# One decoder block on one core: a row normalization taken off GpSimd, row stores moved to GpSimd's queue, one gather ahead of a conditional part, and extra products without readers

## The chip, the cores and the metric

The kernel runs on one core of a Trainium2 chip. The metric is the device time in microseconds of one execution. Times inside an execution are counted from the start of its span. TensorE does matrix products and transposes, VectorE (DVE), ScalarE (ACT) and GpSimd (POOL) work on rows, SyncE (SP) issues most transfers; GpSimd issues the gathers and a few more.

## The reference, cut to what matters

A decoder block for 512 tokens of 1024 channels: a mixer of two parts, a layer norm of `ALPHA * x + mix`, a mixture of 16 experts, a second layer norm. What matters here is the middle:

```python
h = layer_norm(DEEPNORM_ALPHA * h + mix, ln1_g, ln1_b)        # 512 x 1024
group = top-1 of softmax(t @ router_group_w + router_group_b)  # 4 groups
expert_id = top-2 inside the group                             # 2 of 16 experts per token
h_e = silu(t @ expert_w_gate[e]) * (t @ expert_w_up[e])
y = sum over a token's 2 experts of gate * (h_e @ expert_w_down[e])
h = layer_norm(DEEPNORM_ALPHA * h + y, ln2_g, ln2_b)
```

## The kernel before, in words

The tokens lie in four blocks of 128 (`NT = 4`), one token to a partition, in `HT`. Each product of two fp32 matrices is done as three products of rounded halves (`mm3`, `kmm3`: lines 1222 to 1224 in the expert part), and every weight is split into a high part on ScalarE (L824) and a low part on VectorE (L828).

Between the mixer and the experts stands a stage that is written out by hand as a list of steps (L1010): `c` and `e` are parts of the last product of the mixer, `t` and `l` transposes and products for the router's logits, `f` (`finish`) the first layer norm of block i, `g` (`choose`) its two experts, `r` (`ranks`) the place of each token in its experts' lists, and `w` (`warm`) products of a tile of ones that nobody reads. `finish` splits the columns at `w`: VectorE normalizes the first `w` of them (L960, L969), ScalarE and GpSimd the others (L966 to L968). In the kernel before, blocks 0 to 2 have `w = 384` and block 3 has all 1024 on VectorE. The finished rows then go to a tensor `hD` in memory (L970), by SyncE's queue.

`rank_tokens` (L1043, L1045) makes `idx`, a list of up to 128 tokens for each expert. `gather(e)` (L1061) is an indirect transfer on GpSimd's queue that brings an expert's rows from `hD` into one of five buffers `XG`. Two of them, `gather(0)` and `gather(1)`, stand ahead of a conditional part (`tc.If(most > CAP)`, L1095), which serves experts with more than 128 tokens. With the inputs of this kernel it is jumped over. Each engine loads the count `most` (L1092) and branches by itself.

After it come the experts. `turn(e, hh)` transposes half of an expert's gathered rows (L1200) and splits them into `XGH` (ScalarE, L1202) and `XGL` (VectorE, L1203); `gate_up(e, part)` has 12 products (L1222 to L1224, whose third reads `XGL`), `down(e, n)` 6 more for each n. The order in the program is `turn(0, 0)`, `turn(0, 1)`, `gate_up(0, 0)`, eight small products for the gates (L1294), `turn(1, 0)`, `gate_up(0, 1)`, `turn(1, 1)`, and then the loop over experts, which begins with `gate_up(1, 0)`.

The order on an engine is found by a scheduler. An instruction in `K(...)` stays behind the one that the program has before it on its engine; `tc.issue_after(x)` puts what its block has on x's engine behind x. Other instructions may move, also past the conditional part. So `turn(1, 0)` stands behind the products of L1294, and `gate_up(0, 1)` behind `turn(1, 0)`. `eload` (L806, L807, L810) loads 1 MB of expert weights by SyncE's queue into the next of 16 places; a place comes free as its last reader on TensorE is done.

Of the kernel before, what the change touches and what calls it, by code (L numbers as in the profile page):

```python
# [14 lines left out]
I32 = mybir.dt.int32  # L15
AF = mybir.ActivationFunctionType
ALU = mybir.AluOpType
AX = mybir.AxisListType

D = 1024  # L20
S = 512
NT = 4
H = 8
KT = 8
NE = 16
# [5 lines left out]
CAP = 128  # L31
# [5 lines left out]
def body(ctx: ExitStack, tc: tile.TileContext, P: dict, out):  # L37
# [757 lines left out]
    def eload():  # L795

        n = nload[0]
        if n >= len(order):
            return
        nload[0] += 1  # L800
        e, part = order[n]
        kb = at[n] = free.popleft()
        if part < 2:
            raw, lo = both(kb, 4, 512)
            ks = slice(part * 512, part * 512 + 512)
            SP.dma_start(raw[:, :, 0:FF], P["expert_w_gate"][0][e][ks].rearrange("(k p) f -> p k f", p=128))  # L806
            SP.dma_start(raw[:, :, FF:512], P["expert_w_up"][0][e][ks].rearrange("(k p) f -> p k f", p=128))  # L807
        else:
            raw, lo = both(kb, 2, D)
            last_load[0] = SP.dma_start(raw, P["expert_w_down"][0][e].rearrange("(k p) d -> p k d", p=128))  # L810
        raws[order[n]] = raw, lo
# [137 lines left out]

    def finish(i):  # L950

        w = 384 if i < NT - 1 else D
        plt[i] = pb()
        K(T.transpose(plt[i][:, :20], lgT, ident[:20, :20]))
        c = slice(i, i + 1)
        V.bn_aggr(mv[:, i], st[:, i, 0:2 + (i == NT - 1)])
        A.activation(lns[:, c], mv[:, i, 1:2], AF.Sqrt, bias=eps1)
        V.tensor_scalar(lnt[:, c], mv[:, i, 1:2], -0.5, -0.5 * LN_EPS, op0=ALU.mult, op1=ALU.add)
        a, b = HT[:, i, 0:w], HT[:, i, w:D]
        V.scalar_tensor_tensor(a, a, mv[:, i, 0:1], LNR[:, 0, 0:w], op0=ALU.subtract, op1=ALU.mult)  # L960
        V.reciprocal(rst[:, c], lns[:, c])
        V.tensor_scalar(lna[:, c], rst[:, c], rst[:, c], lnt[:, c], op0=ALU.mult, op1=ALU.mult)
        V.tensor_scalar(rst[:, c], lna[:, c], 1.5, rst[:, c], op0=ALU.add, op1=ALU.mult)
        V.scalar_tensor_tensor(nmr[:, c], mv[:, i, 0:1], -1.0, rst[:, c], op0=ALU.mult, op1=ALU.mult)
        if w < D:
            A.activation(b, b, AF.Identity, scale=rst[:, i:i + 1], bias=nmr[:, i:i + 1])  # L966
            G.tensor_tensor(b, b, LNR[:, 0, w:D], ALU.mult)
            G.tensor_tensor(b, b, LNR[:, 1, w:D], ALU.add)  # L968
        V.scalar_tensor_tensor(a, a, rst[:, i:i + 1], LNR[:, 1, 0:w], op0=ALU.mult, op1=ALU.add)  # L969
        stored[i] = SP.dma_start(hD[i * 128:(i + 1) * 128], HT[:, i])  # L970

    def choose(i):

# [32 lines left out]

    stored, plt = {}, {}
    for step in """c0a t00 t10 t01 c0b l00 l10 l01 t11 t20 t30 c1a l11 l20 l30 t02 t03 t21 t31 c1b l02 l03 l21 l31 c2a f0 g0 t12  # L1010
                   t13 c2b l12 l13 r0 e0a f1 g1 t22 t23 e0b l22 l23 r1 e1a f2 t32 e1b g2 l32 r2
                   t33 l33 f3 g3 w8 r3""".split():
        kind, v = step[0], [int(x) for x in step[1:3] if x.isdigit()]
        if kind == "c":
            out_half(1, v[0], int(step[2] == "b"))
        elif kind == "e":
            out_half(1, NT - 1, int(step[2] == "b"), slice(v[0] * 256, v[0] * 256 + 256))
        else:
            {"t": transposes, "l": logits_part, "f": finish, "g": choose, "r": ranks, "w": warm}[kind](*v)
    eload()  # L1020
    with tc.issue_after(stored[NT - 1].ins):
        eload()

    nxt = [2]

# [23 lines left out]
    for i in range(NT):  # L1049
        K(T.matmul(p[:, 0:16], ones_b, EA[:, i], start=i == 0, stop=i == NT - 1))  # L1050
    rank_tokens(idx, RO)
    cmx = rt(1)
    V.tensor_reduce(cmx, p[:, 0:16], axis=AX.X, op=ALU.max)
    cmi = cst(1, dt=I32)
# [7 lines left out]
                                        in_offset=bass.IndirectOffsetOnAxis(ap=idx[:, e:e + 1], axis=0))  # L1062

    earlier = esplit(0, True)
    gather(0)
    second = gather(1)


    gt = cst(NT, 2)
# [17 lines left out]


    yO = dram.tile([(NBLK - 1) * NE * CAP, D], F32, name="yO")
    iD = dram.tile([NE * (NBLK - 1), CAP, 1], I32, name="iD")  # L1090
    with tc.issue_after(second.ins):
        most = nc.values_load(cmi[0:1, 0:1], min_val=0, max_val=S,  # L1092
                              skip_runtime_bounds_check_because="a count of tokens")
# [1 line left out]
    with tc.If(most > CAP):  # L1095
        OW, OX, OXT, OY = reg(40, 2048), reg(192, D), reg(48, KT, 128), reg(192, D)
        OS, OFT = reg(52, FF), reg(53, FF)
        ORO = reg(48, NT, 2, 128, dt=BF16)
        oidx, ork, oi = cst(NBLK - 1, 16, dt=I32), cst(NT, 2), cst(1, dt=I32)
        V.tensor_scalar(gto, rk2, float(CAP), None, op0=ALU.is_ge)  # L1100
        V.tensor_tensor(gto, gt, gto, ALU.mult)
        for b in range(1, NBLK):
            V.tensor_scalar(ork, rk2, float(CAP * b), None, op0=ALU.subtract)
            for i in range(NT):
                rank_one_hot(ORO, ork, i)
            rank_tokens(oidx[:, b - 1], ORO)
            SP.dma_start(iD.rearrange("(e b) p o -> p b (e o)", b=NBLK - 1)[:, b - 1], oidx[:, b - 1])
        with tc.For_i(0, NE, 1) as eo:
            wex = lambda nm, r: P[nm][0][bass.ds(eo, 1)].rearrange("o (k p) f -> p (o k) f", p=128)[:, r]
            for b in range(1, NBLK):  # L1110
                SP.dma_start(oi, iD[bass.ds(eo * (NBLK - 1) + (b - 1), 1)].rearrange("b p o -> p (b o)"))
                G.indirect_dma_start(out=OX, out_offset=None, in_=hD,
                                     in_offset=bass.IndirectOffsetOnAxis(ap=oi[:, 0:1], axis=0))
                for hh in range(2):
                    p = pb()
                    for u in range(4):
                        k = hh * 4 + u
                        T.transpose(p[:, u * 128:(u + 1) * 128], OX[:, k * 128:(k + 1) * 128], ident)
                    V.tensor_copy(OXT[:, hh * 4:hh * 4 + 4], v3(p))
                p = pa()  # L1120
                OGU = OW.rearrange("p (k f) -> p k f", f=512)
                for hh in range(2):
                    ks = slice(hh * 4, hh * 4 + 4)
                    SP.dma_start(OGU[:, :, 0:FF], wex("expert_w_gate", ks))
                    SP.dma_start(OGU[:, :, FF:512], wex("expert_w_up", ks))
                    for k in range(4):
                        T.matmul(p, OXT[:, hh * 4 + k], OGU[:, k], start=hh + k == 0, stop=hh * 4 + k == KT - 1)
                A.activation(OS, p[:, 0:FF], AF.Silu)
                V.tensor_tensor(OS, OS, p[:, FF:512], ALU.mult)
                p = pb()  # L1130
                for f in range(2):
                    T.transpose(p[:, f * 128:(f + 1) * 128], OS[:, f * 128:(f + 1) * 128], ident)
                V.tensor_copy(OFT, p[:, 0:256])
                OD = OW.rearrange("p (k d) -> p k d", d=D)
                SP.dma_start(OD, wex("expert_w_down", slice(0, 2)))
                for n in range(2):
                    p = pa()
                    ns = slice(n * 512, (n + 1) * 512)
                    for f in range(2):
                        T.matmul(p, OFT[:, f * 128:(f + 1) * 128], OD[:, f, ns], start=f == 0, stop=f == 1)  # L1140
                    V.tensor_copy(OY[:, ns], p)
                SP.dma_start(yO[bass.ds(eo * ((NBLK - 1) * CAP) + (b - 1) * CAP, CAP)], OY)
        osl, oslf = cst(NT, 2, dt=I32), cst(NT, 2)
        V.tensor_scalar(oslf, rk2, float(-CAP), 0.0, op0=ALU.add, op1=ALU.max)
        V.scalar_tensor_tensor(oslf, eid, float((NBLK - 1) * CAP), oslf, op0=ALU.mult, op1=ALU.add)
        V.tensor_copy(osl, oslf)
        for i in range(NT):
            for n in range(2):
                G.indirect_dma_start(out=OX, out_offset=None, in_=yO,
                                     in_offset=bass.IndirectOffsetOnAxis(ap=osl[:, i, n:n + 1], axis=0))  # L1150
                V.scalar_tensor_tensor(HT[:, i], OX, gto[:, i, n:n + 1], HT[:, i], op0=ALU.mult, op1=ALU.add)
# [2 lines left out]
    SGB = cst(FF)  # L1154
    later = esplit(1, True)
    behind = V.memset(gto[:, 0, 1:2], 0.0)
    with tc.issue_after(behind.ins):
        earlier()
        K(V.memset(SGB[0:4], 0.0))
# [117 lines left out]
    eps2 = cst(1)  # L1277
    G.memset(eps2, EPS2)
    eload()
    gather(2)  # L1280
    zeros = K(SP.dma_start(yD[ZROW:ZROW + 1].rearrange("o (a b) -> (o a) b", b=FF), SGB[0:4]))
    with tc.issue_after(zeros.ins):
        eload()
    later()
    turn(0, 0)
    turn(0, 1)
    splits()
    gate_up(0, 0)
    gather(3)
    gather(4)  # L1290
    p = pb()
    for i in range(NT):
        for n in range(2):
# [155 lines left out]
```

## Time and profile before

| | us |
|---|---|
| median of 3 runs (lowest to highest) | 817.82 (815.65 to 819.18) |
| the profiled execution: time, span | 816.56, 814.9 |
| busy in the span: PE, DVE, ACT, POOL | 774.1, 536.9, 383.6, 113.1 |
| mean granted TensorE clock | 0.983 |

The profile shows one execution. The span goes from its first to its last instruction; 1.66 us of the execution's time lie around it. An engine that is busy all the time in a stretch bounds it only if others wait for it there. PE's matrix products overlap, so their ends are modelled. A granted clock of 1.00 is 2.4 GHz and 0.50 is 1.2 GHz; a stretch with a value between them had both.

### The profile page before, as it was taken

The numbers are of one execution on the slowest core, as the hardware profiler recorded it, in microseconds if no ns is written. First come the engines' busy times: TensorE is split into PE (matmuls) and PEld (weight loads), VectorE is DVE, ScalarE is ACT, GpSimd is POOL, SyncE is SP. The second block draws the span as 40 slices with busy tenths as digits, with TensorE's granted clock in tenths as the row PEclk, the third lists the DMA queues.
The fourth block names the chain that finished last, engine by engine and source line by source line (L and its number), as shares of the span: only waits on it lengthen the run. The fifth ranks groups of instructions, "written<-read, shape, count | busy, mean of one in ns | idle before, by whom it ended". The sixth has DMA issues, their size and how long they took to land. (4 is left out here: it accounts for less than half of the span.)

```text
span 814.9 us, 10880 instructions
## 1 busy us (share of the span) xinstructions
PE 774.1 (95%) x4043; PEld 642.3 (79%) x4043; DVE 536.9 (66%) x1005; ACT 383.6 (47%) x640; POOL 113.1 (14%) x104
## 2 busy tenths in 40 slices
PE   8999999999999999999999999999985999999990
PEld 7678888888889988887888888888764788888780
DVE  3558954996567974356632322334498999999987
ACT  3545663452245535323322322222325889999833
POOL 2030001000100000002410100000131102100276
PEclk9999999999999999999999999999996999999996
DMA  9970045435540244233444223399628999999762
GB/s 234 219 219 9 1 77 131 81 82 124 86 96 2 57 104 104 69 92 98 126 108 119 88 88 93 103 317 336 224 79 285 321 382 386 370 345 292 284 229 103
DMA packets 105840, 133.65 MB, mean 164 GB/s; under 512 B 18532, under 2 KB 87576, under 8 KB 105784
## 3 DMA queue, kind: packets, MB, share of 16 engines
q1 hardware_dynamic: 101432, 118.08, 49.8%
q0 software_dynamic: 4352, 14.84, 5.4%
q8 instruction: 33, 0.54, 0.3%
q14 instruction: 23, 0.19, 0.1%
HBM read 120.82 MB, written 12.08 MB: 163 GB/s over the span
## 5 line engine op out<-in xcount | busy, mean ns | idle before, releaser
L240 PE MATMUL pa<-r,r 128*128 128x512 f32 (+1 forms) x688 | 268.2, 390 | 0.7 <-DVE r L150 0.7
L239 PE MATMUL pa<-r,r 128*128 128x512 f32 (+1 forms) x688 | 268.8, 391 | 0.0
L241 PE MATMUL pa<-r,r 128*128 128x512 f32 (+1 forms) x688 | 267.6, 389 | 1.1 <-DVE r L150 1.1
L150 DVE TENSOR_TENSOR r<-r,r 128x2048 fp32r<-128x2048 f32 (+2 forms) x51 | 103.6, 2033 | 135.7 <-ACT r L149 135.1
L149 ACT ACTIVATE r<-r 128x2048 fp32r<-128x2048 f32 (+2 forms) x51 | 85.7, 1684 | 141.7 <-PE pa L240 80.7
L241 PEld LDWEIGHTS pa<-r,r 128*128 128x128 f32 x688 | 129.3, 188 | 27.3 <-DVE r L150 1.6
L239 PEld LDWEIGHTS pa<-r,r 128*128 128x128 f32 x688 | 129.4, 188 | 26.3 <-issue 0.9
L240 PEld LDWEIGHTS pa<-r,r 128*128 128x128 f32 x688 | 129.3, 188 | 26.3 <-DVE r L150 1.0
L828 DVE TENSOR_TENSOR r<-r,r 128x1024 fp32r<-128x1024 f32 x96 | 117.0, 1222 | 4.9 <-ACT r L824 2.9
L824 ACT ACTIVATE r<-r 128x1024 fp32r<-128x1024 f32 x96 | 96.3, 1059 | 0.0
L1222 PE MATMUL pa<-r,r 128*128 128x512 f32 x192 | 78.1, 407 | 0.0
L1224 PE MATMUL pa<-r,r 128*128 128x512 f32 x192 | 75.8, 395 | 1.0 <-DVE r L1324 1.0
L1223 PE MATMUL pa<-r,r 128*128 128x512 f32 x192 | 75.6, 394 | 0.0
L398 DVE SCALAR_TENSOR_TENSOR r<-pa,r,r 128x509 f32<-128x509 f32 (+2 forms) x72 | 53.4, 745 | 13.2 <-ACT r L396 12.4
L1224 PEld LDWEIGHTS pa<-r,r 128*128 128x128 f32 x192 | 36.0, 188 | 9.9 <-DVE r L1324 1.9
L1222 PEld LDWEIGHTS pa<-r,r 128*128 128x128 f32 x192 | 36.2, 189 | 7.1 <-ACT r L1202 0.2
L1223 PEld LDWEIGHTS pa<-r,r 128*128 128x128 f32 x192 | 36.3, 189 | 6.9
L399 ACT ACTIVATE r<-r 128x512 f32<-128x512 f32 x24 | 15.1, 629 | 40.2 <-DVE r L398 34.8
L1061 POOL DMA_INDIRECT r<-hD,r x16 | 19.7, 1232 | 91.6 <-PE pb L1200 36.0
L777 POOL TENSOR_TENSOR r<-r,r 128x512 f32<-128x512 f32 x8 | 10.3, 1293 | 144.8 <-DVE r L776 140.6
L396 ACT ACTIVATE r<-pa,r 128x512 f32<-128x512 f32 x24 | 16.3, 685 | 26.7 <-PE pa L241 26.6
L1200 PE MATMUL pb<-r,r 128*128 128x128 f32 x128 | 20.1, 283 | 7.4 <-DVE r L1173 7.3
(336 smaller groups left out, 928.7 us busy)
## 6 DMA issues: line engine op xcount, KB each, us to landing
r<-in_w_in_dram SPq DMA_DIRECT2D x26, 1024.0 KB, 8.6
r<-in_expert_w_gate_dram SPq DMA_DIRECT2D x32, 512.0 KB, 7.6
r<-in_expert_w_down_dram SPq DMA_DIRECT2D x16, 1024.0 KB, 9.2
r<-in_expert_w_up_dram SPq DMA_DIRECT2D x32, 512.0 KB, 8.4
r<-in_w_in_dram SPq DMA_DIRECT2D x12, 512.0 KB, 12.6
yD<-r SPq DMA_DIRECT2D x12, 512.0 KB, 9.9
r<-in_x_dram SPq DMA_DIRECT2D x8, 512.0 KB, 6.2
r<-in_w_dn_out_dram SPq DMA_DIRECT2D x4, 1024.0 KB, 5.0
```

The source lines that it names most:

```text
L149: pin(A.activation(hi, raw, AF.Copy))
L150: pin(eng.tensor_tensor(lo, raw, f_(hi), ALU.subtract))
L239: pin(T.matmul(o, lh, rh, start=first, stop=False))
L240: pin(T.matmul(o, lh, rl, start=False, stop=False))
L241: pin(T.matmul(o, ll, rh, start=False, stop=last))
L398: V.scalar_tensor_tensor(acc[:, s:], p[:, :S - s], wc(3 - s), acc[:, s:], op0=ALU.mult, op1=ALU.add)
L824: K(A.activation(hi[:, s], raw[:, s], AF.Copy))
L828: K(V.tensor_tensor(lo[:, s], raw[:, s], f_(hi[:, s]), ALU.subtract))
L1200: K(T.transpose(p[:, u * 128:(u + 1) * 128], XG[e % 5][:, k * 128:(k + 1) * 128], ident))
L1222: K(T.matmul(args[0], args[1], args[3], start=args[5], stop=False))
L1223: K(T.matmul(args[0], args[1], args[4], start=False, stop=False))
L1224: K(T.matmul(args[0], args[2], args[3], start=False, stop=args[6]))
```

## The change

1. `finish` gives all 1024 columns to VectorE for block 2 as well as for block 3.
2. The rows of all four blocks go to `hD` by GpSimd's queue. The second weight load behind the list of steps is no longer queued behind the last of these stores.
3. `gather(0)` alone stands ahead of the conditional part; `gather(1)` to `gather(4)` are queued on GpSimd behind a small write (`gbehind`) to a tile that the conditional part writes.
4. Inside the conditional part, the loops over the three further lists of an expert are loops of the program and no longer written out.
5. `warm`: 10 products in place of 8 in the list of steps, 8 behind `rank_tokens`, 12 in front of `turn(0, 0)`.

```diff
     def finish(i):
-        w = 384 if i < NT - 1 else D
+        w = 384 if i < NT - 2 else D
...
-        stored[i] = SP.dma_start(hD[i * 128:(i + 1) * 128], HT[:, i])
+        G.dma_start(hD[i * 128:(i + 1) * 128], HT[:, i])
...
-                   t33 l33 f3 g3 w8 r3""".split():
+                   t33 l33 f3 g3 w10 r3""".split():
...
     eload()
-    with tc.issue_after(stored[NT - 1].ins):
-        eload()
+    eload()
...
     rank_tokens(idx, RO)
+    warm(8)
...
-    gather(0)
-    second = gather(1)
+    second = gather(0)
...
     with tc.If(most > CAP):
...
-        for b in range(1, NBLK):
-            V.tensor_scalar(ork, rk2, float(CAP * b), None, op0=ALU.subtract)
+        V.tensor_copy(ork, rk2)
+        with tc.For_i(0, NBLK - 1, 1) as bo:
+            V.tensor_scalar(ork, ork, float(CAP), None, op0=ALU.subtract)
             for i in range(NT):
                 rank_one_hot(ORO, ork, i)
-            rank_tokens(oidx[:, b - 1], ORO)
+            rank_tokens(oidx, ORO)
...
         with tc.For_i(0, NE, 1) as eo:
-            for b in range(1, NBLK):
+            with tc.For_i(0, NBLK - 1, 1) as bo:
...
     behind = V.memset(gto[:, 0, 1:2], 0.0)
+    gbehind = G.memset(gto[:, 1, 0:1], 0.0)
...
     eload()
-    gather(2)
+    with tc.issue_after(gbehind.ins):
+        gather(1)
+        gather(2)
...
     later()
+    warm(12)
     turn(0, 0)
     turn(0, 1)
     splits()
     gate_up(0, 0)
-    gather(3)
-    gather(4)
+    with tc.issue_after(gbehind.ins):
+        gather(3)
+        gather(4)
```

## Rows read from the trace of the kernel before

**Rows 1.** Busy time by stretch: PE, PEld, DVE, ACT, POOL; granted clock; DMA share; GB/s.
```profile
619.60:627.00 7.40, 0.07 (x1) 0.10 (x2) 5.92 (x28) 3.80 (x6) 2.08 (x2) 0.53 0.88 315
627.00:631.00 4.00, 4.00 (x24) 3.20 (x25) 3.88 (x7) 2.69 (x4) 0.94 (x1) 0.59 0.74 237
...
660.00:680.00 20.00, 20.00 (x99) 16.48 (x99) 19.39 (x22) 18.50 (x26) 2.54 (x2) 1.00 1.06 391
```
**Rows 2.** Timeline of VectorE (start, us, line, shapes).
```profile
602.09 0.61 DVE L960 SCALAR_TENSOR_TENSOR r<-r,r,r 128x384 f32<-128x384 f32 x1
...
606.68 1.63 DVE L980 TENSOR_TENSOR r<-r 128x80 f32<-128x80 f32 x1
608.35 1.58 DVE L981 TENSOR_TENSOR r<-r,r 128x80 f32<-128x80 f32 x1
...
612.77 1.27 DVE L960 SCALAR_TENSOR_TENSOR r<-r,r,r 128x1024 f32<-128x1024 f32 x1
...
614.79 1.28 DVE L969 SCALAR_TENSOR_TENSOR r<-r,r,r 128x1024 f32<-128x1024 f32 x1
...
616.60 0.24 DVE L980 TENSOR_TENSOR r<-r 128x80 f32<-128x80 f32 x1
...
619.63 0.17 DVE L1045 CAST r<-pb 128x16 int32<-128x16 f32 x1
...
629.61 1.27 DVE L1203 TENSOR_TENSOR r<-pb,r 128x512 fp32r<-128x512 f32 x2
```
**Rows 3.** Timeline of GpSimd.
```profile
606.65 1.57 POOL L967 TENSOR_TENSOR r<-r,r 128x640 f32<-128x640 f32 x1 [6.72 <-ACT r L966]
...
620.63 1.11 POOL L1061 DMA_INDIRECT r<-hD,r  x1 [10.80 <-DVE r L1080]
622.04 0.97 POOL L1061 DMA_INDIRECT r<-hD,r  x1 [0.30 <-DVE r L1083]
629.89 0.94 POOL L1061 DMA_INDIRECT r<-hD,r  x1 [6.88 <-DVE r L828]
```
**Rows 4.** Timeline of SyncE's queue.
```profile
616.10 0.34 SPq L970 DMA_DIRECT2D hD<-r  x1
616.49 0.42 SPq L810 DMA_DIRECT2D r<-in_expert_w_down_dram  x1
```
**Rows 5.** Transfers: size, us from issue to landing (third: the load of L202).
```profile
hD<-r SPq DMA_DIRECT2D x1, 512.0 KB, 3.1
gcd<-r POOLq DMA_DIRECT2D x1, 16.0 KB, 5.2
...
DMA to landing us min/median/max: 8.5/8.5/8.5
...
r<-hD,r POOLq DMA_INDIRECT x1, 5.6
```
**Rows 6.** The conditional's line L1095: count, ns min/median/max, first and last start.
```profile
L1095 POOLq EVENT_SEMAPHORE  x4: 17/43/43, 621.6 to 628.0; - x4
...
L1095 PEldq COMPARE_BRANCH  x1: 5132/5132/5132, 620.2 to 620.2; - x1
...
L1095 POOLq INC_SWDGE_SEM  x1: 507/507/507, 628.1 to 628.1; - x1
```
**Rows 7.** Timeline of TensorE.
```profile
613.48 3.53 PE L228 MATMUL pb<-r 128*128 128x128 f32 x16
...
618.29 0.17 PE L996 MATMUL pb<-r,r 128*128 128x16 bf16 x1 [1.22 <-DVE r L988]
...
626.93 1.94 PE L1200 MATMUL pb<-r,r 128*128 128x128 f32 x8 [7.33 <-DVE r L1173]
...
630.09 0.71 PE L1200 MATMUL pb<-r,r 128*128 128x128 f32 x4
630.56 0.48 PE L1224 MATMUL pa<-r,r 128*128 128x512 f32 x1
...
636.12 0.48 PE L1222 MATMUL pa<-r,r 128*128 128x512 f32 x1
```

More of the change, by code (lines that the diff above doesn't have):

```diff
@@ L1003, in ranks @@
         V.tensor_scalar(TE[:, i, :, 1], EO[:, i], pid, None, op0=ALU.mult)
-    stored, plt = {}, {}
+    plt = {}
     for step in """c0a t00 t10 t01 c0b l00 l10 l01 t11 t20 t30 c1a l11 l20 l30 t02 t03 t21 t31 c1b l02 l03 l21 l31 c2a f0 g0 t12
                    t13 c2b l12 l13 r0 e0a f1 g1 t22 t23 e0b l22 l23 r1 e1a f2 t32 e1b g2 l32 r2
-                   t33 l33 f3 g3 w8 r3""".split():
-        kind, v = step[0], [int(x) for x in step[1:3] if x.isdigit()]
+                   t33 l33 f3 g3 w10 r3""".split():
+        kind, v = step[0], [int(step[1:])] if step[0] == "w" else [int(x) for x in step[1:3] if x.isdigit()]
         if kind == "c":
@@ L1089, in body @@
     yO = dram.tile([(NBLK - 1) * NE * CAP, D], F32, name="yO")
-    iD = dram.tile([NE * (NBLK - 1), CAP, 1], I32, name="iD")
+    iD = dram.tile([(NBLK - 1) * NE, CAP, 1], I32, name="iD")
     with tc.issue_after(second.ins):
@@ L1098, in body @@
         ORO = reg(48, NT, 2, 128, dt=BF16)
-        oidx, ork, oi = cst(NBLK - 1, 16, dt=I32), cst(NT, 2), cst(1, dt=I32)
+        oidx, ork, oi = cst(16, dt=I32), cst(NT, 2), cst(1, dt=I32)
         V.tensor_scalar(gto, rk2, float(CAP), None, op0=ALU.is_ge)
         V.tensor_tensor(gto, gt, gto, ALU.mult)
-        for b in range(1, NBLK):
-            V.tensor_scalar(ork, rk2, float(CAP * b), None, op0=ALU.subtract)
+        V.tensor_copy(ork, rk2)
+        with tc.For_i(0, NBLK - 1, 1) as bo:
+            V.tensor_scalar(ork, ork, float(CAP), None, op0=ALU.subtract)
             for i in range(NT):
                 rank_one_hot(ORO, ork, i)
-            rank_tokens(oidx[:, b - 1], ORO)
-            SP.dma_start(iD.rearrange("(e b) p o -> p b (e o)", b=NBLK - 1)[:, b - 1], oidx[:, b - 1])
+            rank_tokens(oidx, ORO)
+            SP.dma_start(iD[bass.ds(bo * NE, NE)].rearrange("e p o -> p (e o)"), oidx)
         with tc.For_i(0, NE, 1) as eo:
             wex = lambda nm, r: P[nm][0][bass.ds(eo, 1)].rearrange("o (k p) f -> p (o k) f", p=128)[:, r]
-            for b in range(1, NBLK):
-                SP.dma_start(oi, iD[bass.ds(eo * (NBLK - 1) + (b - 1), 1)].rearrange("b p o -> p (b o)"))
+            with tc.For_i(0, NBLK - 1, 1) as bo:
+                SP.dma_start(oi, iD[bass.ds(bo * NE + eo, 1)].rearrange("b p o -> p (b o)"))
                 G.indirect_dma_start(out=OX, out_offset=None, in_=hD,
@@ L1141, in body @@
                     V.tensor_copy(OY[:, ns], p)
-                SP.dma_start(yO[bass.ds(eo * ((NBLK - 1) * CAP) + (b - 1) * CAP, CAP)], OY)
+                SP.dma_start(yO[bass.ds(eo * ((NBLK - 1) * CAP) + bo * CAP, CAP)], OY)
         osl, oslf = cst(NT, 2, dt=I32), cst(NT, 2)
```

## The prediction

> **What bounds the kernel now.** I read the table of busy time by stretch first, then the timelines of the engines around the change, and last the landings of transfers and the line of the conditional part. The table [rows 1] shows the expert part at 660 to 680 us with TensorE busy for 20.00 of 20.00 us at a granted clock of 1.00. VectorE, ScalarE and the transfers are nearly as full. So TensorE sets the pace there, and whatever makes the first products of expert 1 earlier or later moves the end by as much. The change touches nothing behind that point except the order of a few gathers. Its worth is therefore read from one number: when does the product that now starts at 636.12 us [rows 7] start?
>
> The stretch ahead of it looks idle on TensorE (0.07 us of 7.40, clock 0.53 [rows 1]), but VectorE was busy for 5.92 us of it, and for 3.88 of the next 4.00. In the timeline VectorE goes almost without a gap from 600 us to the split of expert 0's rows, 629.61 us [rows 2], and the first product that needs this split runs at 630.56 us [rows 7]. TensorE came from the other side to the same moment: its transposes at 626.93 us had waited for the first gather, issued at 620.63 us [rows 3], and ran at the lower clock. Two chains thus end within about half a microsecond of each other, and a gain on one alone is worth little.
>
> **Normalization of block 2.** Removed from GpSimd: two instructions of 1.57 us [rows 3]. While they ran, two VectorE instructions of 128x80 took 1.63 and 1.58 us, which take 0.24 us in block 3, where GpSimd is still [rows 2]. That gives back 2.73 us (the second counted at 0.24 too). Added on VectorE: 1024 columns in place of 384 in two instructions, 1.27 for 0.61 us [rows 2] and as much again in the other, in all 1.33 us. VectorE loses no wait in between that would hide this, so its chain from there on is 2.73 - 1.33 = 1.40 us earlier: `idx`, ready at 619.80 us, comes at 618.40; the split of 629.61 at 628.21. If the two slow instructions stayed slow for another reason, this term would be +1.33; if VectorE hid the added columns, -2.73. I take -1.40, since the slow pair stands exactly beside GpSimd's instructions.
>
> **Products without readers.** 16 records took 3.53 us at 613.48 [rows 7], 0.22 each. Two more products are 4 records, at most 0.88 us; TensorE waits for 1.22 us just behind them, at 618.29 us [rows 7], so they cost nothing (0.88 - 1.22 < 0; without that cover, 0.88). The other 20 products are 40 records: at 0.22 us each 8.8, at half of that with the clock up 4.4 us. They run in the hole from 619.6 to 626.9 us, now from about 618.2 to between 622.6 and 627.0. The transposes of expert 0 follow; VectorE will not take them before 628.21 us, and at full clock they need less than the 1.94 us they took. So this is hidden by VectorE's chain. What the higher clock gives (the clock was 0.59 from 627 to 631 us [rows 1]) is hidden by it too.
>
> **Stores by GpSimd's queue.** The last store now starts at 616.10 us [rows 4], right after VectorE's 614.79 + 1.28 us [rows 2], and lands after 3.1 us [rows 5]. On GpSimd it starts at 614.67. No row shows a plain store of 512 KB there. From below: SyncE's 3.1 us. From above: the kernel's first load by this queue, in many short pieces, 8.5 us. Between them stands the only store to memory by GpSimd, 16 KB in 5.2 us [rows 5]. I take 5.2, as that is the same queue and direction: landing at 619.87, 0.7 us after the old one, although issued 1.4 us sooner.
>
> The Trainium skill ("DMA: Bandwidth & Descriptors", section Specifications) gives a first-byte latency of about 1 us for GpSimd's path and 0.6 us for SyncE's. By that page, as an estimate, this store would land after 3.5 us and the sum below would be about 0.0 instead of +0.9; it names SyncE for plain stores, which speaks against this move.
>
> Behind the old stores on SyncE stood weight loads (the one of 616.49 us [rows 4] and its fellow). They go some 6 us earlier. Nobody waits for them, as they belong to experts 4 and 5; they leave the transfers quieter when the gather runs. On GpSimd's queue only `gather(0)` stands behind the last store.
>
> **The gather in front.** It needs `idx` and the last store. `idx` alone would let it go at 618.40 plus the 0.83 us that it took before (619.80 to 620.63), 619.2; the store at 619.87 + 0.30, the usual gap between two of GpSimd's transfers [rows 3], 620.2. So 620.2. Alone on the transfer engines it should land in the 5.6 us of the quickest gather [rows 5], at 625.8, against about 626.6 before. That is 0.8 us on TensorE's side, hidden as said.
>
> **The gather behind the conditional.** Here I see the new wait. GpSimd's waits at the conditional ended at 628.0 us [rows 6], which is where the second gather, issued at 622.04 [rows 3], must have landed: `gather(2)` could only be issued at 629.89, 1.85 us later, with 0.51 us of a semaphore instruction between. In the changed kernel GpSimd waits there for one gather, until 625.8, and `gather(1)` follows at 625.8 + 1.85 = 627.65. With 5.6 us it lands at 633.25; if the memset and the semaphore cost only what they show, some 0.6 us, at 632.0; if the transfer takes 7 us, at 634.7. Before, it had landed at 628.0, ahead of `turn(1, 0)` at 630.09 [rows 7].
>
> Behind `turn(1, 0)` on TensorE stands all of `gate_up(0, 1)`. With VectorE 1.40 earlier, the third product of expert 0 runs at 629.2 and `gate_up(0, 0)` is through at 631.5: 22 products and one transpose group of 0.47 take the 5.56 us from 630.56 to 636.12 [rows 7], 0.23 a product. Then TensorE waits until 633.3. From there: 0.47 for the transposes, 12 x 0.23 = 2.76 for the products, 0.47 for the other transposes, so `gate_up(1, 0)` starts at 637.0. Against 636.12 that is **+0.9 us**.
>
> **The sum.** VectorE's -1.40 and TensorE's clock disappear in a wait that ends 0.9 us later than today. The profiled execution took 816.56 us (span 814.9 and 1.66 around it); it becomes 817.5. The median of the runs is 1.26 us above that execution, so I predict **818.7 us**.
>
> **The rivals.** A difference under 0.5%, about 4.1 us, counts as no change.
>
> *As forecast* (0.45): the wait at `turn(1, 0)`, 817.5 to 820.
>
> *No new wait* (0.20): GpSimd leaves the conditional without waiting for the gather's landing, and `gather(1)` is issued before 625.9, so that it lands before 631.5. Then `gate_up(1, 0)` follows at 631.5 + 0.47 + 2.76 + 0.47 = 635.2, -0.9 to -1.4 us: 816.4 to 816.9. For it: the engine would have no reason of data to wait. Against it: it did so until 628.0 [rows 6].
>
> *The clock falls in the new wait* (0.15): TensorE would stand still from 631.5 to 633.3, and after the hole at 619.6 the lower clock, 1.2 GHz, lasted: 0.59 over 627 to 631 us [rows 1] makes 3.3 of 4 us at half speed. That would cost another 1.6 us: 820.3. Against it: the products without readers keep TensorE busy up to about 625, and 12 products run from 629 to 631.5.
>
> *The stores are late* (0.12), the slower side: if the last store takes 8.5 us as the load of L202 did [rows 5], it lands at 623.2, `gather(0)` goes at 623.5 and lands at 629.1, `gather(1)` lands at 636.6 and `gate_up(1, 0)` starts at 640.3: +4.2 us, 822.0. Each microsecond of that landing behind 5.2 is one of the time; from about 8.4 us on it counts as slower.
>
> *TensorE's branch stays long* (0.08): today it lasts 5.13 us [rows 6] and ends at 625.3, hidden by the first gather. With 8 products ahead of it and 12 behind, the transposes would start at about 629.7, `gate_up(0, 0)` would end at 633.6, and the time would be +1.2: 819.0.
>
> The Trainium skill ("Runtime: NRT & Kernel Launch", section Instruction fetch mechanics) says that a taken branch whose target lies outside the window already fetched has to fetch it first. By that page the part that is jumped over, with its three lists rolled into one, should make this stall vanish; no run so far shows it.
>
> **Range and chances.** The first three cases span 816.4 to 820.3; the runs of the same kernel spread by 1.8 us to each side. 815.0 to 822.0 leaves out the worst of late stores and any gain that no row explains. Slower by over 0.5% needs late stores, alone or with the clock: 0.16. Faster by over 0.5% would need 4.1 us, more than all that VectorE can win back: 0.08. Within 0.5%: 0.76.
>
> **What would show it.** In the changed profile: the two 128x80 instructions of block 2 at 0.24 us; `idx` near 618.4; a last store of about 5.2 us by GpSimd's queue; a branch on TensorE of some 0.1 us; one gather ahead of the conditional and the next near 627.7; TensorE waiting for some 2 us in front of the transposes of `turn(1, 0)`. The prediction is wrong if that wait is missing, if it exceeds 4 us, or if another order of VectorE's instructions moves `idx` by more than the 1.4 us.

## The result, and the profile after

| | before | after |
|---|---|---|
| median (lowest to highest), us | 817.61 (815.65 to 819.18), 4 runs | 823.83 (822.38 to 825.61), 4 runs |
| profiled execution: time, span | 816.56, 814.9 | 825.61, 823.8 |

The ratio is 1.0079, with a 95% interval from 1.0060 to 1.0098: 6.2 us slower, where 0.9 us was forecast and the range ended at 822.0.

**Where to lay the two traces side by side.** GpSimd's last multiplication for block 1 (L968) starts at 598.34 us in the trace of before and at 601.55 us in the one of after, so the profiled execution of after comes 3.21 us late to the stage that was changed. In the profile of a kernel that differs from it by the added products alone (`c2_no_products`, below) the same instruction starts at 598.31 us. Those 3.21 us are thus a matter of that execution, and they are taken off below wherever a time of after is set against one of before. From the first product of expert 1 to the end of the span it is 178.8 us in both (814.9 - 636.12 [rows 7], 823.8 - 644.97). The whole difference lies in between, as the prediction had it.

The timeline of VectorE after the change, which answers to [rows 2]:

```profile
605.31 1.28 DVE L960 SCALAR_TENSOR_TENSOR r<-r,r,r 128x1024 f32<-128x1024 f32 x1
...
611.20 0.24 DVE L980 TENSOR_TENSOR r<-r 128x80 f32<-128x80 f32 x1
611.48 0.24 DVE L981 TENSOR_TENSOR r<-r,r 128x80 f32<-128x80 f32 x1
...
621.29 0.17 DVE L1044 CAST r<-pb 128x16 int32<-128x16 f32 x1 [0.22 <-PE pb L1042]
...
632.09 1.29 DVE L1204 TENSOR_TENSOR r<-pb,r 128x512 fp32r<-128x512 f32 x2 [0.69 <-ACT r L1203]
```

The two slow instructions beside GpSimd are at 0.24 us. `idx` is written at 621.29 + 0.17 - 3.21 = 618.25 us, 1.55 earlier than before. The split of expert 0's rows gains only 0.73 us (632.09 - 3.21 = 628.88 for 629.61), and now it waits for ScalarE, thus for the rows themselves.

SyncE's queue, the first and the last of five weight loads ([rows 4]):

```profile
611.94 0.37 SPq L806 DMA_DIRECT2D r<-in_expert_w_gate_dram  x1
...
614.67 0.51 SPq L807 DMA_DIRECT2D r<-in_expert_w_up_dram  x1
```

GpSimd's timeline from the last store on ([rows 3]):

```profile
618.02 0.53 POOL L970 DMA_DIRECT2D hD<-r  x1 [6.51 <-DVE r L974]
625.67 1.42 POOL L1061 DMA_INDIRECT r<-hD,r  x1 [7.12 <-DVEq L1094]
631.39 0.10 POOL L1157 MEMSET r<- 128x1 f32 x1 [4.30 <-DVE r L828]
632.09 0.97 POOL L1061 DMA_INDIRECT r<-hD,r  x1 [0.59 <-issue]
```

The landing of that store, in the view of transfers ([rows 5]):

```profile
hD<-r POOLq DMA_DIRECT2D x1, 512.0 KB, 6.7
```

The conditional's line, columns as in [rows 6]:

```profile
L1094 POOLq EVENT_SEMAPHORE  x4: 17/43/3970, 626.5 to 630.7; - x4
...
L1094 PEldq COMPARE_BRANCH  x1: 352/352/352, 622.1 to 622.1; - x1
...
L1094 POOLq INC_SWDGE_SEM  x1: 563/563/563, 630.8 to 630.8; - x1
```

The five loads, 3 MB in all, are issued ahead of the last store. The store lands 6.7 us after its issue, and `gather(0)` goes about a microsecond later. The profile puts its 7.12 us of waiting down to a branch on VectorE that took 0.08 us. Where the engine named had long been done, it is another releaser, here the store. Then GpSimd stands at the end of the conditional for 3.97 us, until 630.7, and `gather(1)` goes at 632.09.

TensorE after the change ([rows 7]). `L1201` are the transposes, L1223 to L1225 the three products:

```profile
624.91 2.94 PE L228 MATMUL pb<-r 128*128 128x128 f32 x24 [0.36 <-DVEq L1094]
630.80 1.09 PE L1201 MATMUL pb<-r,r 128*128 128x128 f32 x8 [2.94 <-DVE r L1165]
632.11 0.80 PE L1223 MATMUL pa<-r,r 128*128 128x512 f32 x1 [0.22 <-ACT r L1203]
632.71 0.63 PE L1224 MATMUL pa<-r,r 128*128 128x512 f32 x1
633.14 0.54 PE L1299 MATMUL pb<-r,r 128*128 128x48 bf16 x8
636.41 1.09 PE L1201 MATMUL pb<-r,r 128*128 128x128 f32 x4 [2.73 <-DMA r<-hD,r]
637.15 0.78 PE L1225 MATMUL pa<-r,r 128*128 128x512 f32 x1
637.72 0.63 PE L1223 MATMUL pa<-r,r 128*128 128x512 f32 x1
638.15 0.63 PE L1224 MATMUL pa<-r,r 128*128 128x512 f32 x1
...
644.28 0.39 PE L1225 MATMUL pa<-r,r 128*128 128x512 f32 x1
...
644.97 0.47 PE L1223 MATMUL pa<-r,r 128*128 128x512 f32 x1
```

The granted clock ahead of the steady state, in the windows of [rows 1] moved by 3.2 us (the third is new):

```profile
622.80:630.20 7.40, 4.70 (x33) 4.21 (x31) 6.01 (x25) 3.38 (x4) 1.42 (x1) 0.86 0.49 163
630.20:634.20 4.00, 2.66 (x18) 1.77 (x18) 2.49 (x4) 2.74 (x4) 1.91 (x3) 0.69 0.81 253
634.20:643.20 9.00, 6.79 (x21) 5.56 (x22) 3.43 (x6) 2.06 (x4) 2.94 (x3) 0.57 0.50 173
663.20:683.20 20.00, 20.00 (x99) 16.56 (x98) 19.68 (x22) 18.51 (x27) 4.79 (x3) 1.00 1.07 382
```

Two lines carry the result. `turn(1, 0)` starts at 636.41 - 3.21 = 633.20 us, 3.11 later than its 630.09 [rows 7]. From there to the first product of expert 1 it is 8.56 us (644.97 - 636.41), where before it was 6.03 (636.12 - 630.09), with the same 22 products and two groups of transposes. 3.11 + 2.53 = 5.64 us, against 6.2 in the medians. The 2.53 are the clock: products follow each other at 0.43 us (638.15 - 637.72) and not at 0.23, and the granted clock of that window is 0.57, so most of it ran at 1.2 GHz. Just before, TensorE had waited for 2.94 us, worked from 630.80 to 633.68 and waited for another 2.73 us. The same view by the microsecond (TensorE's busy time and records, granted clock, DMA share, GB/s) shows when the clock fell, and that it came back only near 642 us:

```profile
630.00:631.00 1.00, 0.20 (x2) 1.00 0.83 240
631.00:632.00 1.00, 0.89 (x8) 0.85 0.96 302
632.00:633.00 1.00, 0.89 (x2) 0.50 0.99 341
...
641.00:642.00 1.00, 1.00 (x4) 0.53 0.00 0
```

### The profile page after: what moved, and what is told of

It is laid out like the page before. It is cut to its first block, busy times and chain, and to the rows that moved or that the text cites. A ratio compares the mean times of both kernels' runs of the same rounds, so it can differ in the third digit from the quotient of the medians.

```text
span 823.8 us, 10963 instructions
## 1 busy us (share of the span) xinstructions
PE 782.8 (95%) x4087; PEld 650.6 (79%) x4087; DVE 535.0 (65%) x1005; ACT 382.2 (46%) x639; POOL 114.5 (14%) x107
## 5 line engine op out<-in xcount | busy, mean ns | idle before, releaser
L828 DVE TENSOR_TENSOR r<-r,r 128x1024 fp32r<-128x1024 f32 x96 | 117.1, 1222 | 6.2 <-ACT r L824 4.6
L1223 PE MATMUL pa<-r,r 128*128 128x512 f32 x192 | 79.2, 412 | 0.2 <-ACT r L1203 0.2
L1225 PE MATMUL pa<-r,r 128*128 128x512 f32 x192 | 76.7, 400 | 1.4 <-DVE r L1329 1.4
L1224 PE MATMUL pa<-r,r 128*128 128x512 f32 x192 | 76.0, 396 | 0.0
L1225 PEld LDWEIGHTS pa<-r,r 128*128 128x128 f32 x192 | 36.6, 191 | 10.5 <-DVE r L1329 2.3
L1223 PEld LDWEIGHTS pa<-r,r 128*128 128x128 f32 x192 | 36.8, 192 | 7.2 <-ACT r L1203 0.5
L1061 POOL DMA_INDIRECT r<-hD,r x16 | 22.7, 1420 | 84.2 <-PE pb L1201 38.5
L1203 ACT ACTIVATE r<-pb 128x512 fp32r<-128x512 f32 x32 | 19.0, 598 | 22.4 <-PE pb L1201 14.8
```

The source lines that it names most:

```text
L828: K(V.tensor_tensor(lo[:, s], raw[:, s], f_(hi[:, s]), ALU.subtract))
L1061: return G.indirect_dma_start(out=XG[e % 5], out_offset=None, in_=hD, in_offset=bass.IndirectOffsetOnAxis(ap=idx[:, e:e + 1], axis=0))
L1223: K(T.matmul(args[0], args[1], args[3], start=args[5], stop=False))
L1224: K(T.matmul(args[0], args[1], args[4], start=False, stop=False))
L1225: K(T.matmul(args[0], args[2], args[3], start=False, stop=args[6]))
```

## The experiments

All kernels compute the whole reference. "Stage" is the time from the start of L968's instruction for block 1 on GpSimd, about 600 us, to the first product of expert 1, in the one profiled execution of each. It holds all that the change touches and needs no shift between traces. The medians are set against the kernel before in the same series of runs (817.61 us for the changed kernel, 817.09 for a, 817.43 for c, 817.72 for d and e).

| kernel | stage, us | against before | median, us | against before | ratio, 95% interval |
|---|---|---|---|---|---|
| before | 37.78 | | | | |
| after | 43.42 | +5.64 | 823.83 | +6.2 | 1.0060 to 1.0098 |
| a1_stores_by_sp | 42.46 | +4.68 | 821.63 | +4.5 | 1.0033 to 1.0064 |
| a2_two_gathers_ahead | 39.95 | +2.17 | 819.94 | +2.9 | 1.0011 to 1.0045 |
| a3_both_undone | 36.12 | -1.66 | 816.05 | -1.0 | 0.9974 to 0.9998 |
| a4_products_ahead | 40.04 | +2.26 | 819.73 | +2.6 | 1.0017 to 1.0043 |
| c1_loads_behind | 42.87 | +5.09 | 821.26 | +3.8 | 1.0035 to 1.0075 |
| c2_no_products | 43.24 | +5.46 | 823.81 | +6.4 | 1.0074 to 1.0112 |
| c3_block2_alone | 36.99 | -0.79 | 815.99 | -1.4 | 0.9975 to 0.9998 |
| c4_a3_no_products | 36.93 | -0.85 | 816.34 | -1.1 | 0.9981 to 1.0004 |
| d1_stores_alone | 39.52 | +1.74 | 819.68 | +2.0 | 1.0003 to 1.0036 |
| d2_one_gather_alone | 42.90 | +5.12 | 824.43 | +6.7 | 1.0054 to 1.0105 |
| d3_stores_by_sp_12_ahead | 39.11 | +1.33 | 818.78 | +1.1 | 0.9995 to 1.0028 |
| e1_loads_behind_two_ahead | 36.08 | -1.70 | 816.89 | -0.8 | 0.9971 to 1.0008 |

The two columns of differences go together to about 1.6 us: to within that, what the stage lost or won is what the kernel lost or won.

### Undoing one step of the change

**a1_stores_by_sp**: the changed kernel with the stores back on SyncE's queue and the second load behind the last of them.

```diff
-        G.dma_start(hD[i * 128:(i + 1) * 128], HT[:, i])
+        stored[i] = SP.dma_start(hD[i * 128:(i + 1) * 128], HT[:, i])
...
-    eload()
+    with tc.issue_after(stored[NT - 1].ins):
+        eload()
```

> The changed kernel with one part undone: the four row stores go by SyncE's queue again, and the second weight load is queued behind the last of them. Theory (expert 1's rows arrive late for two reasons, each with its own price): the last store lands after some 3 us in place of 6.7, the first gather goes 3.3 us sooner, and as much is won up to where VectorE binds: 818.5 to 820.0 us, against 823.8 for the changed kernel and 817.6 for the one before. Rival A (only the place of the second gather costs): unchanged, 823.8. Rival B (only the stores cost): 816.4 to 817.6.

It gave back less than expected: 821.6 us, where the theory ended at 820.0. Of the four stores the trace has the landing of the third alone, 3.1 us after its issue. `gather(0)` goes at 621.02, but `gather(1)` goes at 627.24, its instruction takes 2.23 us for 0.97, and `turn(1, 0)` waits for 4.63 us, until 633.68. Counted from L968 that is 34.17 us against 34.86 in the changed kernel. So the late store by itself explains only one to two microseconds of the loss.

**a2_two_gathers_ahead**: the changed kernel with `gather(1)` again ahead of the conditional.

```diff
-    second = gather(0)
+    gather(0)
+    second = gather(1)
...
     with tc.issue_after(gbehind.ins):
-        gather(1)
         gather(2)
```

> The changed kernel with one part undone: the second gather stands ahead of the conditional part again, the stores stay on GpSimd's queue. Theory (two reasons): the second gather follows the first by 1.4 us in place of 6.4, the transposes of expert 1 wait less, 817.5 to 819.5 us. Rival A (only the place of the second gather costs): 816.4 to 817.6. Rival B (only the stores cost): unchanged, 823.8.

This takes back more than half of the loss and ends just above the expected range. What is left is the store: it lands after 7.1 us, the gathers go at 624.62 and 626.37, and both groups of transposes are late together.

**a3_both_undone**: a1 and a2 in one. What is left of the change is block 2's normalization, the rolled loops and the products without readers.

> The changed kernel with both undone: stores by SyncE, two gathers ahead of the conditional part. What is left of the change is block 2's normalization on VectorE, the rolled conditional part and the products without readers. Theory: nothing is late any more and VectorE's 1.4 us come through: 816.2 to 817.6 us. Rival C (the products without readers or the rolled part hold TensorE up by themselves): 819 us or more.

Faster than before by 1.0 us, with an interval below 1.

**a4_products_ahead**: the changed kernel with one alteration of order on TensorE. The small products for the gates stay at their place in the program, so that the first 12 products of `gate_up(0, 0)` run ahead of them and of `turn(1, 0)`.

```diff
-            T.matmul(p[:, 0:48], RO[:, i, n], GB[:, i, n].rearrange("p a b -> p (a b)"),
-                     start=i + n == 0, stop=i == NT - 1 and n == 1)
+            K(T.matmul(p[:, 0:48], RO[:, i, n], GB[:, i, n].rearrange("p a b -> p (a b)"),
+                       start=i + n == 0, stop=i == NT - 1 and n == 1))
```

> The changed kernel, all of it, but the eight small products for the gates are kept in program order, so that on TensorE all 12 products of gate_up(0, 0) stand ahead of the transposes of turn(1, 0) in place of 2. Theory (behind the late transposes stand 22 products, 10 of which could run in the wait): 2.3 us less at the full clock and up to 4 at the lower, 819.8 to 821.5 us. Rival D (the wait ends where it ends and the work behind it is hidden elsewhere): unchanged, 823.8.

Its timeline of TensorE; twelve products run from the first line to the one ahead of L1299, and the wait has shrunk to 1.40 us:

```profile
630.88 0.79 PE L1223 MATMUL pa<-r,r 128*128 128x512 f32 x1
...
634.09 0.39 PE L1225 MATMUL pa<-r,r 128*128 128x512 f32 x1
634.32 0.37 PE L1299 MATMUL pb<-r,r 128*128 128x48 bf16 x8
636.09 0.63 PE L1201 MATMUL pb<-r,r 128*128 128x128 f32 x4 [1.40 <-DMA r<-hD,r]
636.48 0.47 PE L1223 MATMUL pa<-r,r 128*128 128x512 f32 x1
```

From `turn(1, 0)` to expert 1 it is now 639.79 - 636.09 = 3.70 us in place of 8.56, although the gathers go as late as in the changed kernel. The second lands later, so that `turn(1, 0)` itself comes 1.48 us later, counted from L968, and 3.38 of the 4.86 us saved behind it are left. The clock had fallen here too (0.73 over 630 to 634 us), but it was back before the twelve products were through: the products behind `turn(1, 0)` are 0.23 us apart, and the granted clock is 1.00 from 634 us on, 2.4 GHz.

### The loads and the products

**c1_loads_behind**: the changed kernel with three of the weight loads queued behind a small write further on, so that none runs beside the last store.

```diff
-    eload()
-    eload()
...
     with tc.issue_after(zeros.ins):
-        eload()
+        for _ in range(4):
+            eload()
```

> The changed kernel with its stores on GpSimd's queue and its gathers as they are, but the three weight loads that run ahead of the conditional part (2.5 MB, issued by SyncE from 611.9 to 615.2 us) are issued behind it, with the next one. Theory F (the last store is late because these loads are no longer held back behind it and share the transfer engines with it): it lands after some 3.3 us, like the first three stores, the first gather goes 3.4 us sooner, 820.5 to 822.0 us. Rival (GpSimd's queue itself is slow for the last store): 6.7 us again, and 823.8.

Landings of the second, third and last store, in this order, in its view of transfers:

```profile
hD<-r POOLq DMA_DIRECT2D x1, 512.0 KB, 3.0
hD<-r POOLq DMA_DIRECT2D x1, 512.0 KB, 3.4
hD<-r POOLq DMA_DIRECT2D x1, 512.0 KB, 2.9
```

The last store lands after 2.9 us, so it was the loads beside it that made it late, not GpSimd's queue. The time hardly gains: `gather(0)` goes at 620.33 and `gather(1)` at 626.78, but now the loads run beside the second gather, and `turn(1, 0)` waits for it until 634.83, for 5.57 us.

**c2_no_products**: the changed kernel with 8 products in the list of steps again and without the other 20.

```diff
-                   t33 l33 f3 g3 w10 r3""".split():
+                   t33 l33 f3 g3 w8 r3""".split():
...
-    warm(8)
...
-    warm(12)
```

> The changed kernel without its added products that nobody reads (8 in the list of steps, none behind the ranks and none in front of the experts). Theory: they neither delay TensorE nor keep its clock up, because it waits twice for gathered rows behind them: 823 to 825 us, as before the removal 823.8. Rival C (they hold TensorE up): 820 to 822. Rival E (they kept the clock up for the first transposes and that counted): 825.5 or more.

No difference from the changed kernel: the products without readers neither cost nor give anything there.

**c3_block2_alone**: the kernel before with one line changed, `w = 384 if i < NT - 2 else D`.

> The kernel before with only block 2's normalization moved to VectorE. Theory: VectorE's chain is 1.4 us earlier, TensorE's from the first gather (at the lower clock) about 1 us less, so 0.3 to 1.2 us come through: 815.9 to 816.8 us against 817.1 for the kernel before. Rival (the added columns cost as much as GpSimd's port took): 817.1 or more.

Faster by 1.4 us. `idx` comes 1.56 us earlier than before (618.14 us, with L968 at 598.24), and the transposes of expert 0 start at 624.67 for 626.93.

**c4_a3_no_products**: a3 without the added products, by the same edit as c2.

> The kernel with stores by SyncE and two gathers ahead (816.05 us), without the added products: only block 2's normalization and the rolled conditional part are left of the change. Theory: with rows in time the transposes of expert 0 run at the lower clock again, as in the kernel before, and 0.3 to 1 us is lost against 816.05: 816.3 to 817.1. Rival (the products do nothing here either): 816.05.

0.3 us above a3, which the intervals don't tell apart. The transposes of expert 0 take 1.94 us there and 1.06 in a3, but little of that reaches the end.

### One step alone, and the forecast's own kernel

**d1_stores_alone**: the kernel before with `G.dma_start` for the four stores, and the second load free.

> The kernel before with one part of the change: the four stores to hD by GpSimd's queue, and the second weight load no longer behind the last store. Theory (the loads that run ahead make the last store late, as in the changed kernel): the last store lands 6 to 7 us after its issue, gather(0) is issued near 624 us instead of 620.6, and the time is 819.0 to 821.5. Rival (a store on GpSimd's queue is as quick as one on SyncE's and the loads do no harm): it lands in 3 to 3.5 us and the time is that of the kernel before, 817.4 give or take 1.

As the theory had it: the last store goes at 618.25 and `gather(0)` at 624.88, and the time is 2.0 us more (the store's landing is missing from this trace). Counted from L968 the first gather is 2.5 us later than before, and with both gathers ahead of the conditional most of that reaches the end.

**d2_one_gather_alone**: the kernel before with `gather(0)` alone ahead of the conditional and the others behind `gbehind`.

> The kernel before with one part of the change: gather(0) alone ahead of the conditional part, the others behind gbehind. Theory (GpSimd waits at the conditional for gather(0), and 22 products stand behind turn(1, 0) on TensorE, which then also falls to the lower clock): gather(1) is issued near 628 us and lands near 633.5; TensorE waits for 2 to 4 us in front of turn(1, 0), and the time is 820.5 to 823. Rival (GpSimd issues gather(1) early, or the wait is absorbed): 817.4 give or take 1.

6.7 us more, over the theory's upper end. Its timeline of GpSimd:

```profile
621.73 1.11 POOL L1061 DMA_INDIRECT r<-hD,r  x1 [10.80 <-DVE r L1079]
628.25 0.09 POOL L1156 MEMSET r<- 128x1 f32 x1 [5.41 <-DMA r<-in_ln_b_dram]
628.93 1.57 POOL L1061 DMA_INDIRECT r<-hD,r  x1 [0.58 <-issue]
```

And of TensorE:

```profile
630.48 0.54 PE L1297 MATMUL pb<-r,r 128*128 128x48 bf16 x8
634.31 1.09 PE L1200 MATMUL pb<-r,r 128*128 128x128 f32 x4 [3.29 <-DMA r<-hD,r]
635.05 0.78 PE L1224 MATMUL pa<-r,r 128*128 128x512 f32 x1
...
642.35 0.48 PE L1222 MATMUL pa<-r,r 128*128 128x512 f32 x1
```

No store is late here, as `gather(0)` goes 22.28 us behind L968 for 22.29 before, and yet `gather(1)` goes 7.2 us behind `gather(0)`, `turn(1, 0)` waits for 3.29 us, and 8.04 us follow until expert 1. This step alone is as dear as the whole change.

**d3_stores_by_sp_12_ahead**: the edits of a1 and a4 together. This is close to the kernel that the prediction had worked out without knowing it: a store in time, one gather ahead, and 12 products behind `turn(1, 0)`.

> The changed kernel with two of its steps taken back: stores by SyncE's queue with the second load behind the last of them, and the small products for the gates kept in the program's order, so that 12 products of gate_up(0, 0) run ahead of turn(1, 0) and 12, no longer 22, behind it. gather(1) still stands behind the conditional. Theory (two causes add up: the late store and the order on TensorE with the clock): 817.6 to 819.3, gather(0) issued near 621, turn(1, 0) near 633 to 634. Rival (one cause alone sets the time, so that taking both back gives no more than either by itself): 819.7 to 821.6.

818.78 us, +1.1 with an interval that takes in no change at all, where the prediction had 818.7, +0.9. By the times of before (1.25 us off, from L968 at 599.59) the third product of expert 0 runs at 629.26, `turn(1, 0)` at 633.52 and the first product of expert 1 at 637.45; the prediction had 629.2, 633.3 and 637.0. In detail it goes another way: TensorE waits for 2.35 us in front of the third product, for VectorE, runs a part of the products at 0.43 us (the granted clock is 0.50 from 632 to 635 us), and waits only 0.43 us in front of `turn(1, 0)`, where the prediction had 1.8. That the times meet is thus partly luck.

**e1_loads_behind_two_ahead**: the edits of c1 and a2 together. The stores stay on GpSimd's queue.

> The changed kernel with three weight loads queued behind the small writes at the conditional part, so that none runs beside the last store, and with gather(1) ahead of the conditional part again; the stores stay on GpSimd's queue and block 2's normalization on VectorE. Theory (the late store, through the loads, and the gather behind the conditional are all that the change lost): 815.8 to 817.3, the last store landing in 3 to 3.5 us, gathers issued near 620.5 and 622. Rival (GpSimd's queue itself costs something, or the loads that come later delay the gathers or the experts' weights): 818 to 820.

The last store lands after 2.9 us, the gathers go at 619.70 and 621.03, and the loss is gone: -0.8 us, with an interval that just takes in 1. The stage is as short as in a3. No other part of the change loses time that these runs could show.

## Why the prediction was wrong

**Right.** TensorE sets the pace from expert 1 on, and the worth is read from its first product. The normalization gives VectorE 1.40 us: 1.55 by `idx` in the changed kernel, 1.56 in c3. The products without readers cost nothing. GpSimd does wait at the conditional for the first gather. TensorE waits in front of `turn(1, 0)` for 2.73 us, where "some 2 us" were expected, and until 633.20 us, where 633.3 was predicted. The branch on TensorE takes 0.35 us for 5.13 [rows 6]; nothing waited for it before, so that gain is hidden. It takes 0.35 in all ten kernels whose conditional part is rolled, and 3.63 to 5.17 in the four where it is written out. The Trainium skill ("Runtime: NRT & Kernel Launch", section Instruction fetch mechanics) says that a target outside the fetched window costs a fetch; these rows agree, though none shows the fetch itself. The wait is neither missing nor over 4 us, which the prediction had named as signs of its being wrong: what failed lies behind it.

**The step that failed** is the order behind the new wait: "`gate_up(0, 0)` is through at 631.5", so that only 12 products and two groups of transposes, 3.7 us, would stand behind `turn(1, 0)`. In fact TensorE runs two products, those that need `XGH` alone, then the small products and `turn(1, 0)`, and all 22 others behind it. The trace of before has it so: the transposes of 630.09 us stand ahead of the third product at 630.56 [rows 7], and the prediction itself counted 22 products from there. In the program, `turn(1, 0)` is held behind the small products only, and these had been moved ahead of `gate_up(0, 0)`. Ten products at 0.23 us are 2.3 us of work that the prediction put inside the wait and that came behind it. a4 shows the price of this order together with the next point: 3.4 us of stage, 3.6 us in the medians. d3, which has the order that was assumed, comes out at the time that was forecast, though with its waits in other places.

**The clock** was a rival with a chance of 0.15 and a price of 1.6 us: it would fall in the new wait. It cost 2.53 us, and it had fallen before that wait began. It was at 1.00 up to 631 us, all through the first wait, the one for `gather(0)` (627.85 to 630.80), for which the prediction had less than a microsecond (products up to about 625, rows at 625.8). It fell between 631 and 632 us, while TensorE worked, and was at 0.50 when the new wait began at 633.68 and when it ended. The new wait can do the same by itself: in a1 and c1, where `gather(0)` was in time, the clock was 1.00 from 628 to 630 us and 0.50 from 632 on, while TensorE stood in front of `turn(1, 0)`. The argument against the rival was that the products without readers reach to about 625 us and 12 products run from 629 to 631.5. In fact TensorE stood still for 2.94 us behind the former, and two of the latter ran. The order and the clock together are the difference: 8.56 us behind `turn(1, 0)` for 3.70 predicted, 4.86 us, of which 2.3 are the ten products and 2.53 the clock.

**The last store** lands after 6.7 us and not 5.2, and the reason was misjudged: the 5.2 were put down to GpSimd's queue. "They leave the transfers quieter when the gather runs" was right (DMA share 0.03 from 625 to 627 us), but it overlooked that loads which go 6 us earlier run beside the last store. `gather(0)` went at 622.46 by the times of before, and not at 620.2: 1.5 us are the landing, and 0.65 the gap from the landing to the gather, which was 0.95 and not 0.30. That the wait ended where predicted is partly luck: `gather(0)` and `gather(1)` landed after about 5.0 and 4.3 us (625.67 to 630.7, 632.09 to 636.41), less than the 5.6 that were assumed, and made up for most of it. The late store is worth 2.0 us alone (d1), and 1.0 of the stage or 1.7 in the medians behind the later wait (a1). By the Trainium skill ("DMA: Bandwidth & Descriptors", section Specifications) the store would land after some 3.5 us, as an estimate (SyncE's 3.1 us and 0.4 more to the first byte). Without loads beside it (c1, e1) it does: 2.9 to 3.4 us. The same page says, in its section SWDGE vs HWDGE vs iDMA, that a transfer engine takes turns between the queues of both kinds; 6.7 us beside the loads would fit that, but no run here shows the turns.

**What the steps cost alone and together.** The stores alone are +2.0 and the gather alone +6.7, the normalization is -1.4; the sum is 7.3 and the change measures 6.2, which the intervals don't tell apart. Undone in the changed kernel they don't add up: by the stage of the single traces the stores give back 0.96 us, the gather 3.47 and both 7.30. The delays lie on one chain, and where the second gather is late, an earlier first one is worth little: that is why undoing the stores (a1) or moving the loads (c1) gave back only 1.0 and 0.6 us of the stage, 1.7 and 2.4 in the medians, and why a3 and e1 had to undo both.

## What to carry to other kernels

When a new wait is put in front of an instruction, read from the trace of before which instructions stand ahead of it and which behind it on that engine: the program's order doesn't say it, and what stands behind pays for the whole wait, and for a clock that falls during it. A transfer that is moved earlier "because nobody waits for it" has to be checked against every transfer that somebody does wait for. Of the kernels tried, the four without either loss (a3, c3, c4 and e1) lie 0.8 to 1.4 us below the one before and can't be told apart; c3 gets there with one line.

## What the runs showed of the hardware

The instruction that issues a gather on GpSimd takes some 0.95 us at its shortest and up to 2.28 us. In d3 the long ones stand beside VectorE's splits of weights (L828), which read two tiles in the memory that all engines share (`r`); the short one at 629.87 stands beside a split that reads one of its two from TensorE's results (`pb`, L1205). GpSimd:

```profile
627.28 2.28 POOL L1062 DMA_INDIRECT r<-hD,r  x1 [0.58 <-issue]
629.87 0.94 POOL L1062 DMA_INDIRECT r<-hD,r  x1 [0.30 <-DVE r L828]
631.11 1.90 POOL L1062 DMA_INDIRECT r<-hD,r  x1 [0.31 <-issue]
```

VectorE in the same stretch:

```profile
627.38 1.21 DVE L828 TENSOR_TENSOR r<-r,r 128x1024 fp32r<-128x1024 f32 x1
...
628.65 1.21 DVE L828 TENSOR_TENSOR r<-r,r 128x1024 fp32r<-128x1024 f32 x1
629.79 1.27 DVE L1205 TENSOR_TENSOR r<-pb,r 128x512 fp32r<-128x512 f32 x2
630.99 2.46 DVE L828 TENSOR_TENSOR r<-r,r 128x1024 fp32r<-128x1024 f32 x2
```

The Trainium skill ("SBUF — State Buffer", section SBUF: two separate sides) says that a VectorE instruction with two inputs from that memory and a GpSimd instruction that reads it lock each other out of a shared pair of ports, for a whole instruction. These rows agree, but they don't settle it: in the kernel before, a gather issued at 636.52 us took 0.94 us with such splits beside it from 635.42 to 637.90, and no run took the splits away.

A store of 512 KB by GpSimd's queue lands after 2.9 to 3.4 us when no weight load runs beside it, as quickly as by SyncE's queue (2.6 to 4.1 in the kernel before), and after 6.7 to 7.1 us beside five weight loads. And at the end of a conditional part that was jumped over, GpSimd waits for gathers issued ahead of it to land, though no instruction there needs them: 3.97 us in the changed kernel, with one gather ahead, and 6.53 in a2, with two.
